# A two-layer mLSTM and band-attention trunk: row transfers on GpSimd's queue, transposes moved, key inputs scaled by VectorE, and splits put behind bank readers

## The chip, the cores and the metric

The kernel runs on one core of one Trainium2 chip. The metric is the device time of an execution in microseconds, as the median of several runs.

## The reference

The input is 512 tokens of width 2048. Layer 0 is an mLSTM layer with 8 heads, layer 1 attends in chunks of 64 over a band of nine chunks. The keys and values of layer 1 come from the residual stream after layer 0, normalised and modulated anew (`hkv`) and multiplied by `kv_w`. All is float32.

```python
def mlstm_mixer(h, w_in, conv_w, conv_b, gate_b, g_head, w_out):
    proj = h @ w_in
    qk = jax.nn.silu(causal_conv(proj[..., :A_V0].astype(F32), conv_w.astype(F32), conv_b.astype(F32)))
    ...
    gates = proj[..., A_G0:].astype(F32) + gate_b.astype(F32)
    ...
    ht = mlstm_chunkwise(heads(qk[..., :A_QK], A_DK), heads(qk[..., A_QK:], A_DK), heads(v, A_DV), li, lf)
    ht = rmsnorm(ht.transpose(0, 2, 1, 3), g_head.reshape(A_HEADS, A_DV)).reshape(Bn, S, A_INNER)
    y = jax.nn.sigmoid(o.astype(F32)) * ht * jax.nn.silu(z.astype(F32))
    return y.astype(h.dtype) @ w_out

def reference(...):
    for l in range(DEPTH):
        mod = sc @ ada_w[l].astype(F32) + ada_b[l].astype(F32)
        ...
        h = modulate(rmsnorm(x, g_pre[l]), shift, scale).astype(x.dtype)
        if l < N_A_LAYERS:
            y = mlstm_mixer(h, ...)
        else:
            if l == N_A_LAYERS:
                hkv = modulate(rmsnorm(x, kv_g), kmod[:, :D_MODEL], kmod[:, D_MODEL:]).astype(x.dtype)
                kv = hkv @ kv_w
            y = band_attention_mixer(h, k_sh, v_sh, ...)
        x = (x.astype(F32) + gate[:, None, :] * rmsnorm(y, g_post[l])).astype(x.dtype)
```

## The kernel before

Every float32 product is made from three: both factors are split into a high and a low part of the type fp32r (`split`, L247 and L248: ScalarE copies the high part, VectorE subtracts it to get the low one), and `mm` (L316) and `mm3` issue high by high, high by low and low by high into one bank of PSUM. The weights come in pieces of up to 128x1024 in the order in which they are used, always by a load on SP's queue (`raw_load`, L264, tile `wr`); `wpiece` splits a piece into `wh`, and for the projections by seven products (`proj_s`, L365) first forms sums of its blocks on VectorE (`ws`, L287 to L289), which are split into `wsh`. PE multiplies as soon as its piece is there, so PE, ScalarE and VectorE work at neighbouring pieces.

A scheduler sets the order of each engine by priorities. Code under `tc.high_priority(AHEAD)` is put ahead, `behind(a, b)` (L240) puts an instruction behind another in its engine's order without a wait, `pin` keeps program order. A projection takes a table `at` of functions that are called at step `k` of its loop over the 16 input tiles; that is how small work is laid beside products. On an engine, what stands behind a waiting instruction waits too.

The stages that the change touches, in the order of time:

- **Start (to 27 us).** Squares of the input are summed over tokens by PE (`token_sums`), `rc` and the reciprocal give the norm, PE spreads it (`ps_rb`), and the first row tile `h1t` can be made. `awake` (called at L642) issues products that nobody reads, two per call. `ada_sum` (L557) sums one column of the adaLN modulation on VectorE; `early[0]` and `early[1]` are two columns in two halves each, 128x1024.
- **Gates (211 to 250 us).** `gates` (L758) makes the gates' sums in `ps_g`, copies them to `g32`, selects input and forget gate by two products (`ps_li`, `ps_f`), runs log-sigmoid and two scans on VectorE and ScalarE, writes two rows to `gsc`, and transposes `ssum` (its rows `e`) into `aT` by PE (`ps_at`). Behind it head 0's `proj_b` makes the values (`ps_v`).
- **Output of layer 0 and K/V (1400 to 1850 us).** `rows` multiplies by `a_w_out`, in two pairs of row tiles for column groups 2 and 3; `evac` (L1177) multiplies a bank with the gate row `ssum` (loaded by `gate_row`, L1173). `residual` (L1210) adds the input rows and writes the result `y` to `xsc`. `turned` (L1228) normalises four columns' worth (`xn`), transposes them on PE into two banks (`ps_x`), copies each bank to `xk` on ScalarE and writes it to `nsc`. For the first pair of row tiles (`use` false) the key inputs are made later from `xk`, by `key_inputs`; for the second pair (`use` true) at once from the bank. `key_input` (L1220) scales and shifts in place on ScalarE, then splits into `hkv`. `values` (L1366) multiplies with `kv_w` (`ps_kv`) and writes the values to `vsc`. All of these writes and the gate rows are issued by SP.
- **Attention (from about 2040 us).** A head's query and gate come from `proj_s` with four banks D, C, A and B. At its end (L419 to L428) ScalarE reads D, then VectorE reads the banks in the order D, C, C, C, A, B. The next head's `proj_s` takes the banks in turn as they come free.
- **Tail.** `gate_part`, `gate_row(1, 0)` and `gate_first` prepare the last gate row beside `proj_b` of `b_w_out` (`gate_steps`, L1662).

## Time and profile before

| | |
|---|---|
| median of 3 runs | 2621.36 us (2617.01 to 2622.87) |
| profiled execution | 2618.51 us, span 2616.7 us |
| TensorE's clock over the span | 0.999 of full |
| PE busy | 2570.2 us |
| VectorE (DVE) busy | 2324.7 us |
| ScalarE (ACT) busy | 1418.5 us |
| GpSimd (POOL) busy | 57.9 us |

PE's busy time counts matrix products; DVE is VectorE, ACT ScalarE, POOL GpSimd, SP the engine that issues most transfers. An idle time in brackets stands ahead of the instruction that ended it, with what released it.

### The profile page before, as it was taken

Reading aid. Unit: us, or ns where it says so; the run is one execution under the profiler, and the core shown is the slowest. Engines: PE = TensorE matmul, PEld = TensorE weight load, DVE = VectorE, ACT = ScalarE, POOL = GpSimd, SP = SyncE. Lnnn points to the kernel's source line nnn. Section 1 sums busy time; section 2 is a strip of 40 time slices with the busy share of each in tenths; the row PEclk is TensorE's granted clock in tenths of the full one; section 3 lists DMA queues with packets and bytes.
Section 4 is the critical chain, followed back from the end, with each engine's and each line's share of the span. In section 5 each row is a group of like instructions: output and inputs, shape, how many; then the busy total and the mean of one; then the engine's idle time right before and its main releaser. Section 6 shows DMA issues by size and latency. Waiting matters only on the chain. (4 is left out here: it accounts for less than half of the span.)

```text
span 2616.7 us, 45705 instructions
## 1 busy us (share of the span) xinstructions
PE 2570.2 (98%) x17988; PEld 2404.6 (92%) x17988; DVE 2324.7 (89%) x3804; ACT 1418.5 (54%) x2096; POOL 57.9 (2%) x115
## 2 busy tenths in 40 slices
PE   8999999999999999999999999999999999999998
PEld 6887888899999999999999998888999899999887
DVE  8997899999999999999998886877997999999767
ACT  4335534565565555556655442478443776767523
POOL 0000111000000000000000000000000000000000
PEclk9999999999999999999999999999999999999999
DMA  9785597234333343333437558788654544444787
GB/s 366 316 346 198 211 395 297 94 109 141 113 100 135 109 134 112 106 130 114 125 127 249 182 172 330 256 290 282 227 177 145 170 129 145 133 136 134 255 298 251
DMA packets 154019, 506.15 MB, mean 193 GB/s; under 512 B 17750, under 2 KB 31606, under 8 KB 139338
## 3 DMA queue, kind: packets, MB, share of 16 engines
q1 hardware_dynamic: 143482, 442.58, 49.6%
q0 software_dynamic: 10320, 60.65, 6.2%
q8 instruction: 141, 2.31, 0.4%
q14 instruction: 76, 0.61, 0.1%
HBM read 469.50 MB, written 38.90 MB: 194 GB/s over the span
## 5 line engine op out<-in xcount | busy, mean ns | idle before, releaser
L248 ACT CAST wh<-wr 128x1024 fp32r<-128x1024 f32 (+1 forms) x528 | 544.9, 1034 | 483.9 <-DVE wr L288 104.3
L248 DVE TENSOR_TENSOR wh<-wr,wh 128x1024 fp32r<-128x1024 f32 (+1 forms) x528 | 636.3, 1208 | 134.4 <-ACT wh L248 133.5
L248 ACT CAST wsh<-ws 128x768 fp32r<-128x768 f32 (+1 forms) x296 | 241.3, 815 | 294.9 <-PE ps_az L316 60.9
L248 DVE TENSOR_TENSOR wsh<-ws,wsh 128x768 fp32r<-128x768 f32 (+1 forms) x296 | 277.6, 938 | 44.8 <-ACT wsh L248 43.7
L287 DVE TENSOR_TENSOR ws<-wr 128x512 f32<-128x512 f32 (+1 forms) x296 | 199.9, 678 | 8.2 <-DMA wr<-in_wst 7.8
L560 DVE CUSTOM_DVE_ANT_0 ada<-ada,scB,cl 128x2048 f32<-128x2048 f32 (+1 forms) x86 | 199.0, 2323 | 3.6 <-DMA ada<-in_adaT 3.3
L316 PE MATMUL ps_y<-wh,y 128*128 128x512 f32 x768 | 168.6, 380 | 0.0
L316 PE MATMUL ps_y_False<-wh,y 128*128 128x512 f32 x768 | 167.7, 380 | 0.8 <-DVE wh L248 0.8
L316 PEld LDWEIGHTS ps_y_False<-wh,y 128*128 128x128 f32 x768 | 144.5, 189 | 21.8 <-DVE wh L248 1.6
L316 PEld LDWEIGHTS ps_y<-wh,y 128*128 128x128 f32 x768 | 144.3, 189 | 20.7 <-DVE wh L248 0.4
L316 PE MATMUL ps_kv<-wh,hkv 128*128 128x512 f32 x576 | 128.5, 384 | 1.1 <-DVE wh L248 1.0
L316 PE MATMUL ps_v<-wh,h 128*128 128x512 f32 x576 | 127.6, 380 | 0.0
L289 DVE TENSOR_TENSOR ws<-wr 128x256 f32<-128x256 f32 (+1 forms) x296 | 123.5, 420 | 3.2
L316 PEld LDWEIGHTS ps_kv<-wh,hkv 128*128 128x128 f32 x576 | 109.0, 191 | 18.2 <-DVE wh L248 2.9
L288 DVE TENSOR_TENSOR wr<-ws,wr 128x256 f32<-128x256 f32 (+1 forms) x296 | 123.3, 419 | 2.5
L316 PEld LDWEIGHTS ps_v<-wh,h 128*128 128x128 f32 x576 | 108.2, 189 | 15.8 <-issue 0.9
L316 PE MATMUL ps_l<-h,wh 128*128 128x512 f32 x480 | 108.4, 381 | 3.0 <-DVE wh L248 2.1
L316 PEld LDWEIGHTS ps_l<-h,wh 128*128 128x128 f32 x480 | 90.0, 189 | 18.6 <-DVE wh L248 3.5
L316 PE MATMUL ps_azo<-h,wh 128*128 128x256 f32 (+1 forms) x606 | 92.9, 285 | 0.0
L316 PE MATMUL ps_y_True<-wh,y 128*128 128x512 f32 x384 | 83.3, 379 | 0.0
L316 PEld LDWEIGHTS ps_y_True<-wh,y 128*128 128x128 f32 x384 | 72.5, 189 | 10.2
L316 PEld LDWEIGHTS ps_azo<-h,wh 128*128 128x128 f32 x606 | 79.3, 192 | 1.1
(435 smaller groups left out, 5828.7 us busy)
## 6 DMA issues: line engine op xcount, KB each, us to landing
wr<-in_wst SPq DMA_DIRECT2D x498, 512.0 KB, 4.1
ada<-in_adaT POOLq DMA_DIRECT2D x54, 1024.0 KB, 8.6
ada<-in_adaT SPq DMA_DIRECT2D x52, 1024.0 KB, 7.0
ada<-in_adaT SPq DMA_DIRECT2D x36, 512.0 KB, 6.2
wr<-in_wst SPq DMA_DIRECT2D x26, 384.0 KB, 7.5
xt<-nsc SPq DMA_DIRECT2D x32, 256.0 KB, 3.2
yr<-ysc SPq DMA_DIRECT2D x28, 256.0 KB, 5.3
ysc<-zo SPq DMA_DIRECT2D x24, 256.0 KB, 4.5
```

The lines of the kernel that those rows point to most:

```text
L248: ins = nc.scalar.copy(hi, src), nc.vector.tensor_tensor(lo, src, hi.bitcast(F32), op=ALU.subtract)
L287: nc.vector.tensor_tensor(t[:, : 2 * w], r[:, w : 3 * w], r[:, : 2 * w], op=ALU.subtract)
L288: nc.vector.tensor_tensor(r[:, w : 2 * w], t[:, w : 2 * w], r[:, :w], op=ALU.add)
L289: nc.vector.tensor_tensor(t[:, 2 * w :], r[:, 3 * w :], r[:, w : 2 * w], op=ALU.subtract)
L316: product[0] = nc.tensor.matmul(ps, a, b, start=start, stop=stop)
L560: pin(nc.vector.tensor_tensor_reduce(c, c, (sc or scB)[:, j * w : (j + 1) * w], 1.0, mod[:, i : i + 1] if j else col(CB + i), ALU.mult, AL ...
```

## The change

1. The idle pair after the third quarter of the input goes; the first half of `early[1]`'s sum comes ahead of the reciprocal, the second behind the copy of `ps_rb`.
2. `gates` is cut in three: sums and copy (with priority), `gate_rows` at step 2 of head 0's `proj_b`, `gate_cols8` (the transposes) at step 12. Head 0's mask tiles are loaded behind that projection.
3. Layer 0's gate rows, the writes to `xsc` and `nsc`, and those to `vsc` of groups 0 and 1 are issued by GpSimd: 6 loads of `ssum` and 16, 16 and 8 writes, 46 transfers.
4. `key_input` scales on VectorE in place, adds the shift with the rounding copy on ScalarE, and gets the low part by one VectorE instruction that adds the shift and subtracts the high part.
5. `turned` for the first pair moves from steps 8 and 14 of group 2 and 4 and 10 of group 3 to step 10 of group 2 and 0, 6, 12 of group 3; for the second pair from 4, 8, 14 to 4, 10, 14. Its copy and key inputs have priority where the second pair uses them at once.
6. In head 1's `proj_s` the low split of piece 1 and the first block sum of piece 2 are put behind head 0's last reader of bank C (`emptied`), and so are the low splits of the tiles that were kept plain.
7. In the tail three gate steps move by two steps each, and one to the last pair.

```diff
-            nc.vector.tensor_tensor(t[:, : 2 * w], r[:, w : 3 * w], r[:, : 2 * w], op=ALU.subtract)
+            summed[0] = nc.vector.tensor_tensor(t[:, : 2 * w], r[:, w : 3 * w], r[:, : 2 * w], op=ALU.subtract)
...
+        if held_back and i in (1, 2):
+            behind((parted[0], summed[0])[i - 1], emptied[0])
...
-        nc.vector.tensor_tensor(z(z2, 1), z(z1, 1), c1, op=ALU.add)
+        emptied[0] = nc.vector.tensor_tensor(z(z2, 1), z(z1, 1), c1, op=ALU.add)
...
-def ada_sum(i, at, w, js, pin=lambda ins: ins, sc=None):
+def ada_sum(i, at, w, js, pin=lambda ins: ins, sc=None, j0=None):
+    j0 = js[0] if j0 is None else j0
...
-        c = at[:, (j - js[0]) * w : (j - js[0] + 1) * w]
+        c = at[:, (j - j0) * w : (j - j0 + 1) * w]
...
-    if q:
+    if q in (1, 3):
...
+ada_sum(*early[1][:3], [0], pin)
...
-ada_sum(*early[1], pin)
+ada_sum(*early[1][:2], early[1][2], [1], pin, None, 0)
...
-    nc.scalar.copy(like(g32[:32], S), read(g_ps[:32], S))
+    with tc.high_priority(AHEAD):
+        nc.scalar.copy(like(g32[:32], S), read(g_ps[:32], S))
+    return g32
+
+def gate_rows(g32):
...
+
+def gate_cols8():
+    e = ssum[:8]
...
-        gates()
+        g32 = gates()
...
-    nm = hp.tile([P, S], F32, tag="nm", name=f"nm{h}")
-    nmd = hp.tile([P, 4, P], F32, tag="nmd", name=f"nmd{h}")
-    nc.sync.dma_start(nm, gsc[0, h].partition_broadcast(P))
+
+    def mask_tiles():
+        nm = hp.tile([P, S], F32, tag="nm", name=f"nm{h}")
+        nmd = hp.tile([P, 4, P], F32, tag="nmd", name=f"nmd{h}")
+        nc.sync.dma_start(nm, gsc[0, h].partition_broadcast(P))
+        return nm, nmd
...
+        nm, nmd = mask_tiles()
...
+        add_at(at, {2: lambda: gate_rows(g32), 12: gate_cols8})
...
+        nm, nmd = mask_tiles()
...
-    nc.sync.dma_start(gb, ggd[layer, 4 * g : 4 * g + 4, :].rearrange("k p -> (k p)").partition_broadcast(P))
+    (nc.sync if layer else nc.gpsimd).dma_start(gb, ggd[layer, 4 * g : 4 * g + 4, :].rearrange("k p -> (k p)").partition_broadcast(P))
...
-        nc.sync.dma_start(xsc[m, :, d], y)
+        nc.gpsimd.dma_start(xsc[m, :, d], y)
...
-    nc.scalar.activation(tmp, tmp, AF.Identity, bias=mod[:, 96 + k : 97 + k], scale=amul[:, KT + k : KT + k + 1])
+    shift = mod[:, 96 + k : 97 + k]
+    nc.vector.tensor_scalar(tmp, tmp, amul[:, KT + k : KT + k + 1], None, op0=ALU.mult)
...
-    split(hkv[k][:, 0, t], hkv[k][:, 1, t], tmp)
+    hi, lo = hkv[k][:, 0, t], hkv[k][:, 1, t]
+    nc.scalar.activation(hi, tmp, AF.Identity, bias=shift)
+    nc.vector.scalar_tensor_tensor(lo, tmp, shift, hi.bitcast(F32), op0=ALU.add, op1=ALU.subtract)
...
-            nc.scalar.copy(keep, ps)
+            with tc.high_priority(AHEAD if use else 0):
+                nc.scalar.copy(keep, ps)
...
-            nc.sync.dma_start(nsc[k : k + 2, :, t].rearrange("a p t -> p a t"), keep)
+            nc.gpsimd.dma_start(nsc[k : k + 2, :, t].rearrange("a p t -> p a t"), keep)
...
-            if use:
-                for j in range(2):
+            with tc.high_priority(AHEAD if use else 0):
+                for j in range(2 if use else 0):
...
-            at |= {8 + 6 * i: lambda i=i: turned(0, [i], False) for i in range(2)}
+            at[10] = lambda: turned(0, [0], False)
...
-            at = {4 + 6 * i: lambda i=i: turned(0, [2 + i], False) for i in range(2)}
+            at = {6 * i: lambda i=i: turned(0, [1 + i], False) for i in range(3)}
...
-        nc.sync.dma_start(vsc[g][:, :, m * P : (m + 1) * P], v.rearrange("p (j t) -> p j t", j=4))
+        (nc.gpsimd if g < 2 else nc.sync).dma_start(vsc[g][:, :, m * P : (m + 1) * P], v.rearrange("p (j t) -> p j t", j=4))
...
-        turn = {k: lambda i=i: turned(1, [i], True) for i, k in enumerate((4, 8, 14))} if pair == 0 and g == 1 else {}
+        turn = {k: lambda i=i: turned(1, [i], True) for i, k in enumerate((4, 10, 14))} if pair == 0 and g == 1 else {}
...
-    proj_s("b_w_in", h2, h2s, ATT_PAIRS if h else ATT_FIRST, z1, z2, f"z{h}", kq, (2, 2), steps, True, late=True)
+    proj_s("b_w_in", h2, h2s, ATT_PAIRS if h else ATT_FIRST, z1, z2, f"z{h}", kq, (2, 2), steps, True, late=True, held_back=h == 1)
...
-                split(s1[:, 0, :], s1[:, 1, :], raw[0][:, 256:])
+                behind(split(s1[:, 0, :], s1[:, 1, :], raw[0][:, 256:])[0], emptied[0])
...
-    3: {2: lambda: (gate_row(1, 3), fetch_x(3)), 6: lambda: gate_part(0), 8: lambda: gate_row(1, 0, late[1]), 12: lambda: gate_first(0), 14: lambda: gate_first(2)},
+    3: {2: lambda: (gate_row(1, 3), fetch_x(3)), 8: lambda: gate_part(0), 10: lambda: gate_row(1, 0, late[1]), 14: lambda: gate_first(0)},
...
-        at = {4: lambda: finish(0), 6: lambda: finish(1)} if pair == PAIRS[1] else {}
+        at = {2: lambda: gate_first(2), 4: lambda: finish(0), 6: lambda: finish(1)} if pair == PAIRS[1] else {}
```

How the order moves, at three places. PE at the gates, before: `ps_v0` are head 0's values, `wh41` the weight piece.

```order
L316 MATMUL ps_g_1593<-h1_15_1338,gw_1540 32x512 x2
L316 MATMUL ps_v0_0_1668<-wh41_1674,h1_0_269 128x512 x3
L316 MATMUL ps_v0_0_1668<-wh41_1674,h1_1_302 128x512
L316 MATMUL ps_li_1628<-g32_1626,kcs_101 8x512
L316 MATMUL ps_f_1629<-g32_1626,kcs_101 8x512
L316 MATMUL ps_v0_0_1668<-wh41_1674,h1_1_302 128x512 x2
```

And after the change:

```order
L316 MATMUL ps_v0_2_1633<-wh41_1637,h1_1_301 128x512 x3
L316 MATMUL ps_v0_3_1634<-wh41_1637,h1_0_268 128x512 x3
L316 MATMUL ps_v0_3_1634<-wh41_1637,h1_1_301 128x512 x3
L316 MATMUL ps_li_1664<-g32_1625,kcs_101 8x512
L316 MATMUL ps_f_1665<-g32_1625,kcs_101 8x512
L316 MATMUL ps_v0_0_1631<-wh42_1693,h1_2_392 128x512 x3
L316 MATMUL ps_v0_1_1632<-wh42_1693,h1_2_392 128x512 x3
```

The two selecting products moved from behind four products of `wh41` to behind all 24 of them. The transposes `ps_at` stood within `wh44` and stand behind `wh46`:

```order
L316 MATMUL ps_v0_1_1632<-wh46_1812,h1_11_931 128x512 x3
L316 MATMUL ps_v0_2_1633<-wh46_1812,h1_11_931 128x512 x3
L316 MATMUL ps_v0_3_1634<-wh46_1812,h1_11_931 128x512 x3
L804 MATMUL ps_at_1842<-kcs_101,ssum_108 128x8 x4
L316 MATMUL ps_v0_0_1631<-wh47_1850,h1_12_1041 128x512 x3
L316 MATMUL ps_v0_1_1632<-wh47_1850,h1_12_1041 128x512 x3
```

VectorE where layer 0's second pair of rows begins its last column group, before: `xn` are normalised rows, `ps_y0_2_2` and `ps_y0_2_3` banks to be evacuated, `wh338` and `wh339` splits.

```order
L1236 TENSOR_SCALAR xn0_3_17984<-y0_3_16628,rsn_107 128x512
L1236 TENSOR_SCALAR xn1_3_17986<-y1_3_16678,rsn_107 128x512
L248 TENSOR_TENSOR wh338_17878<-wr338_17876,wh338_17878 128x1024
L1179 TENSOR_TENSOR ps_y0_2_2_False_17610<-ps_y0_2_2_False_17610,y2_2_16142 128x512
L1183 TENSOR_TENSOR y2_2_16142<-ps_y0_2_2_False_17610,ssum_108 128x512
L1179 TENSOR_TENSOR ps_y0_2_3_False_17611<-ps_y0_2_3_False_17611,y3_2_16192 128x512
L1183 TENSOR_TENSOR y3_2_16192<-ps_y0_2_3_False_17611,ssum_108 128x512
L248 TENSOR_TENSOR wh339_17919<-wr339_17917,wh339_17919 128x1024
```

After the change:

```order
L1256 TENSOR_SCALAR xn0_3_18007<-y0_3_16627,rsn_107 128x512
L1256 TENSOR_SCALAR xn1_3_18009<-y1_3_16677,rsn_107 128x512
L1241 TENSOR_SCALAR xk0_0_17749<-xk0_0_17749,amul_104 128x256 x2
L248 TENSOR_TENSOR wh338_17877<-wr338_17875,wh338_17877 128x1024
L1196 TENSOR_TENSOR ps_y0_2_2_False_17609<-ps_y0_2_2_False_17609,y2_2_16141 128x512
L1196 TENSOR_TENSOR ps_y0_2_3_False_17610<-ps_y0_2_3_False_17610,y3_2_16191 128x512
L1200 TENSOR_TENSOR y2_2_16141<-ps_y0_2_2_False_17609,ssum_108 128x512
L1200 TENSOR_TENSOR y3_2_16191<-ps_y0_2_3_False_17610,ssum_108 128x512
L248 TENSOR_TENSOR wh339_17898<-wr339_17896,wh339_17898 128x1024
L1246 SCALAR_TENSOR_TENSOR hkv0_17868<-xk0_0_17749,mod_103,hkv0_17868 128x256
L1241 TENSOR_SCALAR xk0_2_17757<-xk0_2_17757,amul_104 128x256 x2
```

The two scalings of `xk0_0` stand ahead of `wh338` and of the evacuations.

VectorE at the end of attention's head 0, before: `wh430`, `ws431` and `wr431` are head 1's weights, `z0` and `zq0` head 0's results, `ps_dz0` and `ps_cz0` the banks D and C.

```order
L248 TENSOR_TENSOR wsh429_0_22026<-ws429_0_22019,wsh429_0_22026 128x768
L248 TENSOR_TENSOR wh430_22077<-wr430_22071,wh430_22077 128x1024
L287 TENSOR_TENSOR ws431_0_22147<-wr431_22145 128x512
L248 TENSOR_TENSOR h2_14_21736<-xt14_0_21683,h2_14_21736 128x256
L288 TENSOR_TENSOR wr431_22145<-ws431_0_22147,wr431_22145 128x256
L420 TENSOR_TENSOR z0_21751<-zq0_21750,ps_dz0_21752 128x256
L289 TENSOR_TENSOR ws431_0_22147<-wr431_22145 128x256
L421 TENSOR_TENSOR zq0_21750<-z0_21751,ps_cz0_21753 128x256
L422 TENSOR_TENSOR z0_21751<-z0_21751,ps_cz0_21753 128x256
L423 TENSOR_TENSOR z0_21751<-zq0_21750,ps_cz0_21753 128x256
```

After the change:

```order
L248 TENSOR_TENSOR wsh429_0_22025<-ws429_0_22018,wsh429_0_22025 128x768
L422 TENSOR_TENSOR z0_21750<-zq0_21749,ps_dz0_21751 128x256
L423 TENSOR_TENSOR zq0_21749<-z0_21750,ps_cz0_21752 128x256
L424 TENSOR_TENSOR z0_21750<-z0_21750,ps_cz0_21752 128x256
L425 TENSOR_TENSOR z0_21750<-zq0_21749,ps_cz0_21752 128x256
L248 TENSOR_TENSOR wh430_22076<-wr430_22070,wh430_22076 128x1024
L426 TENSOR_TENSOR zq0_21749<-zq0_21749,ps_az0_21753 128x512
L428 TENSOR_TENSOR z0_21750<-z0_21750,ps_bz0_21754 128x512
L248 TENSOR_TENSOR wsh430_0_22079<-ws430_0_22072,wsh430_0_22079 128x768
```

The four readers of D and C come first, head 1's split `wh430` behind them, its next weight steps behind those of A and B.

## Rows read from the trace of the kernel before

**Rows 1.** The page, part 1: busy us of each engine, share, instructions.

```profile
PE 2570.2 (98%) x17988; PEld 2404.6 (92%) x17988; DVE 2324.7 (89%) x3804; ACT 1418.5 (54%) x2096; POOL 57.9 (2%) x115
```

**Rows 2.** Waits of PE, whole run: line, releaser; us in total, times, longest.

```profile
PE ps_li L316 <- ACT g L764: 2.3, 1, 2.3
PE ps_gg L839 <- DVE ggate L837: 1.5, 1, 1.5
PE ps_at L793 <- DVE ssum L784: 1.4, 1, 1.4
PE ps_x L1244 <- DVE xn L1236: 1.4, 2, 0.7
```

**Rows 3.** Timeline 16 to 28 us: start, us, instruction, idle before and its releaser.

```profile
17.73 1.20 PE L316 MATMUL ps_idle<-scB,cst 128*128 128x256 f32 x2
22.47 0.18 DVE L648 RECIPROCAL rc<-rc 128x4 f32<-128x4 f32 x1 [2.23 <-ACT rc L645]
22.57 1.25 DVE L560 CUSTOM_DVE_ANT_0 ada<-ada,scB,cl 128x1024 f32<-128x1024 f32 x1
25.44 0.75 DVE L529 SCALAR_TENSOR_TENSOR h1t<-xt,amul,ps_rb 128x512 f32<-128x512 f32 x1 [0.28 <-ACT ssum L655]
```

**Rows 4.** Timeline 209 to 250 us, around the gates.

```profile
213.45 0.56 ACT L764 COPY g<-ps_g 32x512 f32<-32x512 f32 x1
...
244.31 1.23 DVE L248 TENSOR_TENSOR wh<-wr,wh 128x1024 fp32r<-128x1024 f32 x1 [3.95 <-ACT wh L248]
...
248.81 0.55 POOL L554 DMA_DIRECT2D ada<-in_adaT  x1 [4.05 <-DVE mod L560]
```

**Rows 5.** Timeline 1707 to 1720 us, where layer 0's rows are turned.

```profile
1708.01 1.08 ACT L1248 COPY xk<-ps_x 128x512 f32<-128x512 f32 x2 [0.42 <-PE ps_x L1244]
...
1709.61 1.28 DVE L1236 TENSOR_SCALAR xn<-y,rsn 128x512 f32<-128x512 f32 x3
...
1710.10 0.95 SPq L1250 DMA_DIRECT2D nsc<-xk  x2
1710.30 1.04 PE L1244 MATMUL ps_x<-kcs,xn 128*128 128x128 f32 x8
...
1711.10 8.02 PE L316 MATMUL ps_y_False<-wh,y 128*128 128x512 f32 x36
...
1715.95 0.60 ACT L1223 ACTIVATE xk<-xk,mod,amul 128x256 f32<-128x256 f32 x1 [3.38 <-DMA nsc<-xk]
```

**Rows 6.** Timeline 2082 to 2086 us, where attention's second head begins.

```profile
2082.39 0.36 ACT L419 COPY zq<-ps_dz 128x256 f32<-128x256 f32 x1
2082.51 1.22 DVE L248 TENSOR_TENSOR wh<-wr,wh 128x1024 fp32r<-128x1024 f32 x1
...
2084.91 0.42 DVE L420 TENSOR_TENSOR z<-zq,ps_dz 128x256 f32<-128x256 f32 x1
...
2085.39 0.94 PE L316 MATMUL ps_cz<-h2s,wsh 128*128 128x256 f32 x6 [2.82 <-DVE z L420]
```

**Rows 7.** Timeline 1743 and 1773 us: two waits of PE.

```profile
1743.49 1.78 PE L316 MATMUL ps_kv<-wh,hkv 128*128 128x512 f32 x7 [0.62 <-DVE wh L248]
...
1773.25 0.95 PE L1244 MATMUL ps_x<-kcs,xn 128*128 128x128 f32 x4 [2.44 <-DVE hkv L248]
```

**Rows 8.** Windows: length; busy PE, PEld, DVE, ACT, POOL; clock, DMA share, GB/s.

```profile
1740.00:1750.00 10.00, 9.38 (x44) 7.93 (x43) 10.00 (x19) 8.57 (x20) 0.00 (x0) 1.00 0.67 209
...
1770.00:1774.00 4.00, 1.56 (x11) 1.21 (x9) 2.93 (x7) 4.00 (x10) 0.00 (x0) 0.93 0.91 245
1774.00:1784.00 10.00, 10.00 (x46) 8.56 (x45) 5.94 (x9) 6.55 (x13) 0.00 (x0) 0.86 0.66 206
```

**Rows 9.** DMA issues: queue, count, KB each, median us from issue to landing.

```profile
ada<-in_adaT POOLq DMA_DIRECT2D x54, 1024.0 KB, 8.6
...
out<-yo POOLq DMA_DIRECT2D x8, 256.0 KB, 4.0
out<-yo SPq DMA_DIRECT2D x8, 256.0 KB, 2.7
```

More of the change, by code (lines that the diff above doesn't have):

```diff
@@ L311, in wpiece @@
         return out
-    product = [None]
+    product, emptied, summed = [None], [None], [None]
     def mm(ps, a, b, start, stop):
@@ L363, in proj_b, with proj_s @@
             held.clear()
-    def proj_s(mat, xs, ss, f, z1, z2, name, pl, bufs, at={}, merged=False, banks="pppp", lead=AHEAD, late=False):
+    def proj_s(mat, xs, ss, f, z1, z2, name, pl, bufs, at={}, merged=False, banks="pppp", lead=AHEAD, late=False, held_back=False):
         D, C, A, B = [(newa if b == "a" else newp)(f"ps_{n}{name}") for n, b in zip("dcab", banks)]
```

## The prediction

> **What bounds the kernel now.** I read the page's busy times first, then PE's waits over the whole run, then the timeline at the places that the change touches, then the windows for the clock. PE is busy for 2570.2 of 2616.7 us [rows 1], so everything a reordering can win is the 46.5 us in which it is not, plus what a fallen clock costs. A gain counts only where PE stands and the changed step is what it stands for. The waits on the change's own lines are few and each has one place [rows 2]: the gates' first product on ScalarE's copy (2.3 us), the gates' transposes on the chain behind it (1.4), two waits on the normalised rows (1.4 together). Two larger ones lie in the attention and in the shared K/V stage (below). The sum is made against the profiled execution's 2618.5 us, which lies 2.9 below the median of the three runs, 2621.4; a time is given as a median by adding the 2.9 again. About 0.2%, or 5.2 us, is what a measurement of this kernel can tell from no change.
>
> **Start.** One idle pair goes, which held PE for about 1.0 us at 17.73 ahead of the last token sums. The reciprocal at 22.47 ended 2.23 us of VectorE idleness, so VectorE was free at 20.24 [rows 3]. The first half of the adaLN sum (1.25) now goes there and ends at 21.5, just where the reciprocal could start if its input comes 1.0 earlier. VectorE's 0.28 at 25.44 stays a wait for the same copy, which comes earlier too. Gain 0.9; between 0, if the stage that follows is held by its weight loads, and 2.0, if VectorE's 2.2 us of filled idleness is passed on to PE.
>
> **Gates.** ScalarE's copy of the gate sums ends at 213.45 + 0.56 = 214.01 [rows 4], and PE had stood for it for 2.3 us [rows 2], from about 211.7. The product now stands behind 20 further matmuls. Thirty-six of that shape took 8.02 us, 0.223 each [rows 5], so PE gets there 4.5 us later, at 216.2, when the copy is done. The transposes move behind 57 more matmuls, 12.7 us. Their chain starts about 2.2 later than it did (216.2 against 214.01), so some 10 us are in hand over a wait of 1.39. That chain's scans now push the weight splits behind them, but one of these stood 3.95 us for ScalarE at 244.31 [rows 4], so a few us of delay are covered there; if the cover is gone, PE stands at a split instead. Gain 2.30 + 1.39 = 3.7; ends 1.5 (the second wait returns at a split) and 3.7.
>
> **Attention.** PE stood 2.82 us at 2085.39 for the first reader of a bank, which VectorE reached only at 2084.91, behind 1.22 us of head 1's split and three smaller weight steps [rows 6]. ScalarE's copy, which that reader needs, ends at 2082.75. The reader now comes first: 2082.75 + 0.42 = 2083.2, so PE starts 2.2 us earlier. What is late next is head 1's split: it ends at about 2085.6, and PE needs it after 30 of the short matmuls, six of which take at most 0.94 us [rows 6], so 3 to 4.7 us after 2083.2, from 2086.5 on. Two pieces later the splits have hardly any slack, because the scores' operand is now split behind more weight steps, so I take 2.0, with ends 0.8 and 2.8.
>
> **K/V stage.** At 1773.25 PE stood 2.44 us for a bank that key_input had not yet emptied [rows 7], and the granted clock fell to 0.93 and then 0.86 in the windows around it, a mix of 2.4 GHz with some 1.2 GHz, right after that stand [rows 8]: 10 us at 0.86 lose 1.4. The second set of transposes now comes two steps, 12 matmuls or 2.7 us, later, just over the 2.44, and copies and key inputs have priority, so the wait goes and with it, I take it, the fall. Gain 2.44 + 1.4 = 3.8; ends 1.0 (the third set now follows the second after four steps where it had six, and meets the same banks) and 4.2. The 32 scalings that VectorE gains are 128x256. By the 128x512 row (1.28 for three, 0.43 each [rows 5]) that is 0.21 each, and up to 0.42 for those in PSUM, by the equally small row at 2084.91 [rows 6]: 7 to 13 us over a stage where VectorE is idle for over a third of the time (8.87 busy of 14 us from 1770 on [rows 8]). Only 1740 to 1750 is full (10.00 of 10 [rows 8]); PE stood 0.62 there [rows 7], and two such scalings add 0.5. ScalarE's relief is worth nothing there, since VectorE ends last.
>
> **The writes on POOL.** This is the cost that the trace of before does not show. Forty-six transfers leave SP for POOL. The scaling is in place, so it must wait until the write of the same tile to nsc has landed, and now VectorE waits, in its order, ahead of a weight split and of the next evacuations. Before, ScalarE waited: 3.38 us, released at 1715.95 by a write that SP issued at 1710.10, thus 5.85 later [rows 5]. Now the first of the two copies ends at about 1708.6, POOL's issue takes 0.55 [rows 4], and with 5.85 the landing comes 6.4 after the copy, at 1715.0. VectorE is there at 1709.61 + 1.28 = 1710.9 and stands for 4.1 us. Its split then ends at 1715.0 + 0.4 + 1.25 = 1716.65. PE wants it at 1711.10 + 24 x 0.223, less the 0.8 that the transposes moved behind it take (1710.30 to 1711.10) [rows 5]: 1715.65. So PE loses L - 5.4 us there, with L the time from copy to landing: 1.0 at L = 6.4. For the three later pairs VectorE comes some 5.6 us after the copy and has about 1 us in hand over PE, L - 6.6 each, nothing at 6.4. The bounds of L are 4.0 + 0.55, POOL's 256 KB writes of the output, and 8.6 + 0.55, its 1 MB loads [rows 9]; I take SP's figure for the same write, the nearest row. Cost 1.0; ends 0 and 11.4 (3.75 + 3 x 2.55).
>
> The rows of the output's writes speak for a longer L: the same 256 KB took 4.0 on POOL and 2.7 on SP [rows 9], 1.3 more; with 1.3 more here L is 7.7 and the cost 2.3 + 3 x 1.1 = 5.6. A page of the Trainium skill gives a reason against such a move, "SBUF — State Buffer", section "SBUF: two separate sides": GpSimd writes the descriptors of its own DMAs through a port pair that VectorE locks in its two-port modes, and a transfer of 0.62 us alone took 3.1 beside a copy. By that, an estimate, L would be 2.5 longer, 8.9, the cost 10.4 and the time 2621.9. The trace bears out a lengthening of about half that size.
>
> **Steps that I cost at nothing.** The two waits on normalised rows (1.4 [rows 2]) stay: those transposes keep their place in PE's order. The tail's moved gate steps leave every engine's order as it was, so the 1.5 us for the gate row [rows 2] stays too. SP, freed of 46 issues, may bring a weight load forward; no wait of PE in this stage names one.
>
> **Sum.** 0.9 + 3.7 + 2.0 + 3.8 - 0.5 - 1.0 = 8.9 us, so 2609.6 for a profiled execution and 2612.5 as a median.
>
> **Rivals.**
> First, waits that only move: a split behind the gates' chain, head 1's later splits, the third set of transposes. For it speaks that each was covered by only 1 to 4 us of idleness; against it, that the gates' transposes have 10 us in hand. All three at their low ends give 0.9 + 1.5 + 0.8 + 1.0 - 1.5 = 2.7 us: 2618.7, no change that can be told.
> Second, POOL's writes land late while VectorE is busy, between L = 7.7 (the 1.3 of [rows 9]) and the upper bound, 9.15. The whole is then worth 9.9 - 5.6 = 4.3, or 9.9 - 11.4 = -1.5: 2617.1 to 2622.9. For it: POOL was the slower queue in the one pair of rows that compares them; against it: 1.3 is a figure of another stage. The Trainium skill's rule on the shared ports belongs here; its figure lies inside this span.
> Third, the same mechanism carried to the other side, slower: four stands of VectorE, each with a PE stall and a fallen clock behind it. Without the landings the change is worth 9.9. It turns at 4L = 35.1, L = 8.8, and is slower by 5.2 from L = 10.1 on. At L = 10.5 the time is 5.1 + 3 x 3.9 = 16.8 lost, net 6.9: 2628.3. For it: DMA share is 0.91 in the neighbouring window [rows 8], and a 1 MB load on POOL needs 8.6. Against it: these writes are a quarter of that size, and one was seen at 5.85.
> Fourth, the change does not do what it says: for the tail that is so by the order; for the rest the order shows the moves.
>
> **How the numbers follow.** My forecast, the sum with single terms off by one or two us but at least 5.2 in all, 0.66. First rival 0.13. Second 0.14, all of it within 0.2%. Third 0.07. Faster by over 0.2%: 0.66; within: 0.27; slower: 0.07. The forecast's own range is 2607 to 2616, from the high ends of the terms (2.0 + 3.7 + 2.8 + 4.2 = 12.7, and 1.7 for the spread of single runs, which before's show to be larger) to 5.2. The range to hold 8 in 10 takes in the first rival and most of the second: 2607 to 2621.
>
> **What would show it.** Right: no wait of PE on the gates' copy or transposes; PE's wait at the attention's second head down to about 0.6; no wait of PE for a bank near 1773 and a clock of 1.00 there; VectorE standing 3 to 5 us for an nsc write at the first scaling and 0 to 2 at the three others, with PE losing about 1. Wrong: VectorE stands of 6 us and more there; a new wait of PE for a weight split near 235 to 245 or 2090 to 2097; a clock below 1.00 between 1710 and 1740.

## The result, and the profile after

The change made the kernel slower: 2625.45 us as the median of 12 runs (2622.65 to 2629.74) against 2621.36 of 12 runs of the kernel before beside them, ratio 1.0019 with a 95% interval of 1.0011 to 1.0026. Forecast were 2612.5, and 2607 to 2621. The profiled execution has a span of 2623.5 us.

The page's part 1 of the kernel after, to be read against [rows 1]:

```profile
PE 2571.8 (98%) x17986; PEld 2405.1 (92%) x17986; DVE 2335.8 (89%) x3836; ACT 1405.5 (54%) x2063; POOL 87.4 (3%) x161
```

PE is as busy as before, in a span 6.8 us longer; VectorE has 11.1 us more, within the 7 to 13 that were worked out. PE's waits, whole run, as [rows 2]:

```profile
PE ps_kv L316 <- DVE wh L248: 5.1, 7, 1.3
PE ps_x L1264 <- ACT sqy L1203: 3.2, 1, 3.2
PE ps_kv L316 <- ACT wh L248: 2.7, 2, 2.5
PE ps_t L1550 <- DVE s L1541: 2.3, 2, 1.5
...
PE ps_kv L316 <- ACT hkv L1245: 1.6, 1, 1.6
PE ps_gg L850 <- DVE ggate L848: 1.5, 1, 1.5
PE ps_x L1264 <- DVE xn L1256: 1.3, 3, 0.8
```

The waits on the gates' copy and transposes are gone, as is that of attention's bank; those on the tail and on the normalised rows stay, as forecast. New are the waits of the K/V stage (`ps_x` on a square sum, `ps_kv` on weights). Three markers show where the time went. The view of one line's instructions gives their first and last start: the gate of the output norm (first at 294, last at 2584), layer 0's evacuations, and the first keys. Before:

```profile
L837 DVE TENSOR_TENSOR ggate<-mod,cl x5: 155/159/165, 299.3 to 2576.8; 128x4 f32<-128x4 f32 x4, 128x16 f32<-128x16 f32 x1
L1183 DVE TENSOR_TENSOR y<-ps_y_False,ssum x16: 681/684/692, 1604.3 to 1741.6; 128x512 f32<-128x512 f32 x16
L426 DVE TENSOR_TENSOR zk<-zk,ps_bk x2: 679/682/684, 1855.3 to 1875.5; 128x512 f32<-128x512 f32 x2
```

After:

```profile
L848 DVE TENSOR_TENSOR ggate<-mod,cl x5: 154/155/162, 294.0 to 2584.2; 128x4 f32<-128x4 f32 x4, 128x16 f32<-128x16 f32 x1
L1200 DVE TENSOR_TENSOR y<-ps_y_False,ssum x16: 678/682/683, 1599.3 to 1742.9; 128x512 f32<-128x512 f32 x16
L428 DVE TENSOR_TENSOR zk<-zk,ps_bk x2: 679/679/679, 1863.6 to 1883.9; 128x512 f32<-128x512 f32 x2
```

The change is 5.3 us ahead at the first gate and 5.0 at the first evacuation, and 8.3 behind at the first keys: the stage from evacuation to keys takes 264.3 us where it took 251.0, 13.3 more. From the first keys to the last gate it wins 0.9 (720.6 against 721.5). So all of the loss lies in the output and K/V stage. Between its two markers PE stands 16.3 us (264.30 - 248.01) where it stood 6.2 (251.00 - 244.79). The windows of before and after (columns as [rows 8]):

```profile
1604.30:1855.30 251.00, 244.79 (x1217) 213.03 (x1216) 197.93 (x285) 160.16 (x275) 0.00 (x0) 0.99 0.84 283
```

```profile
1599.30:1863.60 264.30, 248.01 (x1213) 213.01 (x1212) 209.44 (x317) 149.94 (x243) 28.92 (x45) 0.99 0.78 268
```

The first part of the loss, in the timeline at 1704 to 1716 us (start, duration, instruction, idle before and its releaser; answers to [rows 5]):

```profile
1703.94 1.08 ACT L1269 COPY xk<-ps_x 128x512 f32<-128x512 f32 x2
...
1704.96 1.60 POOL L1271 DMA_DIRECT2D nsc<-xk  x2 [3.57 <-ACT xk L1269]
...
1711.09 0.62 DVE L1241 TENSOR_SCALAR xk<-xk,amul 128x256 f32<-128x256 f32 x2 [4.28 <-ACT wh L248]
...
1711.62 1.22 DVE L248 TENSOR_TENSOR wh<-wr,wh 128x1024 fp32r<-128x1024 f32 x1
...
1713.95 1.28 DVE L1200 TENSOR_TENSOR y<-ps_y_False,ssum 128x512 f32<-128x512 f32 x2
1714.73 0.58 ACT L1203 ACTIVATE sqy<-ps_y_False 128x512 f32<-128x512 f32 x1 [3.72 <-DVE y L1200]
...
1715.47 1.12 PE L1264 MATMUL ps_x<-kcs,xn 128*128 128x128 f32 x4 [3.25 <-ACT sqy L1203]
```

The first copy ends at 1704.52 (1703.94 + 0.58), the scaling runs at 1711.09: L is 6.6, forecast 6.4, and VectorE stands 4.28 us (4.1). The row names ScalarE's cast, which ended at 1711.00, but the scaling does not read what that cast wrote. What it needs is the write issued at 1704.96, and the view of that write alone says 6.0 us from issue to landing, thus 1711.0:

```profile
DMA to landing us min/median/max: 6.0/6.0/6.0
```

Behind the scaling stand the split and the four evacuation steps, behind these ScalarE's square sum, which is the last reader of a bank, and for that bank PE's next transposes stand 3.25 us. At the later pairs VectorE stands four more times, up to 3.52, and behind the longest PE stands 1.25 for the split that follows the scaling:

```profile
1739.40 0.61 DVE L1241 TENSOR_SCALAR xk<-xk,amul 128x256 f32<-128x256 f32 x2 [3.52 <-DMA nsc<-xk]
...
1741.21 2.86 PE L316 MATMUL ps_kv<-wh,hkv 128*128 128x512 f32 x12 [1.25 <-DVE wh L248]
```

The second part of the loss is near 1800. Windows of the kernel after (columns as [rows 8]):

```profile
1710.00:1720.00 10.00, 6.75 (x30) 5.68 (x29) 8.35 (x14) 5.51 (x12) 1.97 (x3) 0.83 0.54 189
...
1800.00:1810.00 10.00, 7.00 (x30) 5.23 (x29) 5.28 (x11) 6.50 (x10) 0.73 (x1) 1.00 0.95 345
1810.00:1820.00 10.00, 9.38 (x36) 7.97 (x37) 9.93 (x16) 8.63 (x13) 0.71 (x1) 0.83 0.65 217
```

PE loses some 3 us of 10 in two windows, and the granted clock is 0.83, a mix of 2.4 and 1.2 GHz, in the window of the first stand and in the one behind the second: an estimate of up to 2 x 10 x 0.17 = 3.4 us. Before, in [rows 8], the clock fell in this stage only behind the 2.44, by the same reckoning 4 x 0.07 + 10 x 0.14 = 1.7 us.

### The profile page after: what moved, and what is told of

It reads as the page before. It is cut to its first block, busy times and chain, and to the rows that moved or that the text cites. A ratio compares the mean times of both kernels' runs of the same rounds, so it can differ in the third digit from the quotient of the medians.

```text
span 2623.5 us, 45740 instructions
## 1 busy us (share of the span) xinstructions
PE 2571.8 (98%) x17986; PEld 2405.1 (92%) x17986; DVE 2335.8 (89%) x3836; ACT 1405.5 (54%) x2063; POOL 87.4 (3%) x161
## 4 chain that ended last, share of the span: by engine, by line
PE 67%; DVE 21%; issue 7%; DMA 2%; ACT 2%; POOL 1%; SPq 0%; DVEq 0%; ACTq 0%; POOLq 0%
PE ps_y L316 6%; DVE wh L248 5%; PE ps_azo L316 4%; PE ps_czo L316 4%; PE ps_dzo L316 4%; PE ps_y_True L316 3%; PE ps_az L316 3%; PE ps_y_False L316 3%; PE ps_dz L316 3%; PE ps_cz L316 3%; PE ps_o L316 3%; DVE wsh L248 2%; PE ps_l L316 2%; PE ps_v L316 2%; PE ps_bzo L316 2%
## 5 line engine op out<-in xcount | busy, mean ns | idle before, releaser
L316 PEld LDWEIGHTS ps_y_True<-wh,y 128*128 128x128 f32 x384 | 72.6, 189 | 10.2
```

The source lines that it names most:

```text
L316: product[0] = nc.tensor.matmul(ps, a, b, start=start, stop=stop)
```

## Experiments

Times are medians; a ratio is to the kernel before, run beside it; "us of the ratio" is its distance from 1 times 2621.4, and gains and costs below are told in it. For the change itself that is +5.0. The edits are given in short form, with several places of the code in one line.

**Which part.** The change without parts 3 to 5: `key_input`, `turned` and the issues as before.

```diff
-scale on VectorE; turned at {10}, {0, 6, 12}, (4, 10, 14); nc.gpsimd
+scale on ScalarE; turned at {8, 14}, {4, 10}, (4, 8, 14); nc.sync
```

> The change without its K/V part: transfers of layer 0 on SP, key_input on ScalarE, transposes at their old steps, no priority for copies and key inputs. Theory (all of the loss lies in the K/V stage, between pieces 300 and 380 of the weights): start and gates keep their 5 us, the attention its 1, so 5 to 7 us below before, ratio about 0.9975. Rival (the gates' or the attention's part shifts work that costs time later): 0 to 3 us below before.

2617.08, 0.9974 [0.9962, 0.9985]: start, gates, attention and tail are worth 6.8 us. The reverse, the kernel before with parts 3 to 5 alone:

```diff
-scale on ScalarE; turned at {8, 14}, {4, 10}, (4, 8, 14); nc.sync
+scale on VectorE; turned at {10}, {0, 6, 12}, (4, 10, 14); nc.gpsimd
```

> The kernel before with the K/V part alone (transfers on GpSimd, key inputs scaled by VectorE, moved transposes, priorities). Theory: 9 to 13 us above before, ratio 1.004 to 1.005. Rival (the loss needs the shift of 5 us that the earlier parts bring): under 4 us.

2634.16, 1.0039 [1.0026, 1.0052], 10.2 us slower. With the earlier parts the same parts cost 11.8 (5.0 + 6.8), so the loss does not need them. Then the whole change, but all 46 transfers back on SP:

```diff
-nc.gpsimd.dma_start(xsc / nsc / vsc / gate row ...)
+nc.sync.dma_start(...)
```

> The change with all 46 transfers back on SP; scaling in place on VectorE and moved transposes kept. Theory A (the in-place scaling makes VectorE wait for the landing, whichever queue issued the write; SP's write lands 5.9 us after its issue, GpSimd's was waited for some 6.5 us): PE still stands 2 us and more for a bank near 1712, and 0 to 3 us are won on the change. Theory B (GpSimd's queue is the cost): 8 to 12 us are won, 4 to 8 below before, and no wait of PE there.

2613.26, 0.9958 [0.9945, 0.9972]: 11.0 us faster than before. So parts 4 and 5 are worth 4.2 (11.0 - 6.8; the two intervals overlap), and the issues by GpSimd cost 16 us, 0.0061 of the ratio (13 by the medians; these intervals lie well apart). PE's waits from 1650 to 1860 us in this run:

```profile
PE ps_kv L316 <- DVE wh L248: 2.5, 3, 1.0
PE ps_kv L316 <- ACT hkv L1245: 0.9, 1, 0.9
PE ps_x L1264 <- ACT wh L248: 0.8, 1, 0.8
```

No wait for a bank is left, neither the 2.44 of [rows 7] nor the 3.25. The same without the order that part 6 sets:

```diff
-proj_s(..., late=True, held_back=h == 1)
+proj_s(..., late=True)
```

> All transfers on SP (as in the run before that did so), and in the attention head 1's splits no longer held behind head 0's bank readers. Theory (holding wins PE's 2.8 us at the second head, but gives part back at the softmax's transposes): 0 to 2 us slower than with the hold, PE again standing 2 to 3 us for z, and no wait for the softmax's rows. Rival (the hold is worth its full 2 us and more): 2 to 3 us slower.

2615.36, 0.9971 [0.996, 0.9982]. That is 3.4 us for part 6 (1.8 by the medians), but the two intervals overlap, so the size is open. What is plain in the trace is that without it PE stands again, and the clock behind it falls (timeline and window):

```profile
2079.48 1.65 PE L316 MATMUL ps_cz<-h2s,wsh 128*128 128x256 f32 x6 [2.19 <-DVE z L422]
```

```profile
2080.00:2090.00 10.00, 10.00 (x77) 9.94 (x76) 9.49 (x17) 6.15 (x9) 0.00 (x0) 0.87 0.27 83
```

**Which transfers.** One group on GpSimd, the others on SP. The nsc writes alone:

```diff
-nc.gpsimd.dma_start(xsc / vsc / gate row ...)
+nc.sync.dma_start(...)
```

> The change with only the 16 nsc writes on GpSimd; gate rows, xsc and vsc writes back on SP. Theory A (the nsc writes are what is waited for): nearly the whole loss stays, 0 to 3 us won on the change. Theory B (46 transfers in one queue delay each other, the nsc writes behind the xsc and vsc writes): 5 us and more are won, and the wait for nsc at the first scaling is under 2 us.

2619.88, 0.9985 [0.9976, 0.9994], 8.9 better than the change, though the stand at the first scaling is still there: 4.95 us of VectorE, and 4.00 of PE for the square sum's bank. Neither expectation fits whole. The values' vsc writes alone:

```diff
-nc.gpsimd.dma_start(xsc / nsc / gate row ...)
+nc.sync.dma_start(...)
```

> The change with everything on SP (2613.3) but the 8 writes of the values to vsc, which GpSimd issues as in the change. The run with the nsc writes alone on GpSimd (2619.9) was about 6 us faster than the change, most of it between 1800 and 1850. If the values' writes are what costs there (their landings, or the order that they bring about): 2617 to 2619.5, with PE waits for weight splits of 2 us and more near 1807. If the gate rows and xsc writes are: 2612.5 to 2614.5, with the K/V stage as in the run with all on SP. If the loss comes only where these writes and the nsc writes share GpSimd's queue: 2612.5 to 2614.5 here and in the next run as well.

2617.5, 0.9985 [0.9977, 0.9994]. The gate rows and xsc writes alone:

```diff
-nc.gpsimd.dma_start(nsc / vsc ...)
+nc.sync.dma_start(...)
```

> The change with everything on SP (2613.3) but the 6 gate rows and the 16 writes to xsc, which GpSimd issues as in the change. If these cost the 6 us: 2617 to 2619.5, and then a wait of PE for a normalised row or a load of the rows must show between 1690 and 1850. If the values' writes do, or only the sharing of the queue with the nsc writes: 2612.5 to 2614.5.

2616.76, 0.9984 [0.9975, 0.9993]. Each group costs about 7 us against all on SP, with intervals clear of that run's; all three cost 16, less than the sum. The last two expectations had set one group against the other; both cost. Moving only the second pair's eight nsc writes back to SP changes nothing that can be told:

```diff
-nc.gpsimd.dma_start(nsc ...)
+(nc.sync if use else nc.gpsimd).dma_start(nsc ...)
```

> The change with only the second pair's eight nsc writes back on SP. PE's order is the same as the change's. Theory A (the loads of nsc for the attention's input wait for GpSimd's late writes, and ScalarE and VectorE stand for those loads ahead of weight splits): the losses from 1800 to 1850, some 9 us, shrink to under 3, so 5 to 8 us are won on the change; PE's 3.25 us near 1712 stay. Theory B (the loss there comes from the values' writes or from the key inputs' priority): under 2 us.

2626.81, 1.0013 [1.0004, 1.0022]; its first expectation had 5 to 8 us won on the change.

**The nsc writes: landing or order.** First the wait taken away: the first pair's key inputs are scaled into a tile of their own.

```diff
-nc.vector.tensor_scalar(tmp, tmp, ...)
+src, tmp = tmp, rows_p[0].tile([P, w], F32, tag="ks", bufs=1)
+nc.vector.tensor_scalar(tmp, src, ...)
```

> The change with the scaled key input of the first pair written to a scratch tile of its own, so that VectorE need not wait for the write of the tile it reads; transfers on GpSimd. Theory A (the wait for the landing behind the in-place scaling): PE's 3.25 us near 1712 and the low clock after it go, 4 to 6 us are won on the change; the losses from 1800 to 1850 stay. Theory B (GpSimd's queue in general, or the places of the transposes): under 2 us are won.

2621.81, 0.9994 [0.9984, 1.0004], 6.6 us better than the change; PE's wait for the square sum is gone, though PE now stands 1.85 us for a normalised row, up to 1704.59. Then only the order: the first two scalings behind the evacuations, where the kernel with all on SP has them (`emptied` is the last evacuation).

```diff
+behind(scaled, emptied[0])
```

> The change, transfers on GpSimd, but VectorE's first two scalings are put behind the evacuations and weight splits that they stood ahead of, as the scheduler itself places them when SP issues the writes. Theory A (VectorE's place in the order: the scheduler takes GpSimd's writes for landed earlier than they are): PE's 3.25 us near 1712 go and 4 to 6 us are won on the change, as with the scratch tile; the losses from 1800 to 1850 stay. Theory B (GpSimd's queue slows the stage by itself): under 2 us are won.

2624.21, 1.0008 [0.9999, 1.0017], 2.9 better by intervals that overlap, less than the 4 to 6 expected; the 3.25 is gone here too, but PE stands 2.71 us for a normalised row, up to 1705.88. And a step towards the reverse: all on SP, with the split put behind the scaling (`parted` is that split).

```diff
+behind(parted[0], scaled)
```

> The change with everything on SP, and weight split 338 put behind the first scaling on VectorE, as it stands in the change. It tells the order from the queue at 1712. If the order that came with GpSimd is what costs there: PE loses 2 to 4 us near 1712 as in the change (a wait for the square sum's bank or for the split), clock below 1.00 behind it, 2615.5 to 2618. If it is GpSimd's later landing in itself, SP's write lands about 1 us sooner, and PE loses at most 1: 2612.5 to 2615.

2614.46, 0.9971 [0.996, 0.9982], 3.4 us worse than all on SP, with SP's landings. The median falls into the second expectation's range; that PE stands 1.49 us for the split, up to 1714.26, and 1.32 up to 1730.56 speaks for the first. It is not the change's order, though: here three of the four evacuation steps stand ahead of the scaling, in the change all four behind it, and no wait for the square sum's bank shows. PE's longest item from 1650 to 1860 us:

```profile
PE ps_y_False L319 <- DVE wh L248: 3.4, 3, 1.5
```

So this order would be up to half of the 7 us that the nsc writes cost; the intervals of 0.9971 and 0.9958 overlap, so this share is not certain. That the scheduler puts the scaling ahead because its own reckoning frees SP is argued, not shown; the run with gate rows and xsc writes on GpSimd, below, fits it.

**The values' writes: the ring.** In the run with vsc alone on GpSimd, SP's waits and ScalarE's, 1780 to 1850 us:

```profile
SPq L1289 <- DMA vsc<-v: 16.1, 5, 5.4
```

```profile
ACT xt L1423 <- DMA xt<-nsc: 13.7, 7, 3.6
```

With all on SP they were

```profile
SPq L1289 <- DMA vsc<-v: 1.7, 3, 0.7
```

```profile
ACT xt L1423 <- DMA xt<-nsc: 7.0, 7, 2.7
```

The values' tiles `v` share a ring of six buffers with the row tiles `xt`. SP's load of the next `xt` waits until the write of an old `v` has landed, now by another queue, and weight loads stand behind it on SP. The landing is late because GpSimd issues the second of two values' writes late. Timelines of GpSimd in this run, and of SP with all on SP:

```profile
1805.72 0.72 POOL L1399 DMA_DIRECT2D vsc<-v  x1 [20.09 <-ACT v L1398]
1811.47 0.71 POOL L1399 DMA_DIRECT2D vsc<-v  x1 [5.03 <-issue]
```

```profile
1802.65 0.52 SPq L1399 DMA_DIRECT2D vsc<-v  x1
...
1804.35 0.53 SPq L1399 DMA_DIRECT2D vsc<-v  x1
```

The second tile was ready at 1807.03 in the first and its write was issued 4.4 us later. It stood for the first write: the view of that one, issued at 1805.72, gives the time to its landing, thus 1811.2, and the second starts 0.3 us after it.

```profile
DMA to landing us min/median/max: 5.5/5.5/5.5
```

If this is the way, buffers of their own must win it back (`vp` is a pool of four):

```diff
-v = tp.tile([P, S], F32, tag="t", ...)
+v = vp.tile([P, S], F32, tag="v", ...)
```

> As the run with the values' writes alone on GpSimd (2617.5), but the values of groups 0 and 1 have four buffers of their own, not the ring of six that the row tiles use. If SP's stand for those writes (16.1 us, five times, up to 5.4) is the way in which they cost: SP's waits on vsc are gone, ScalarE's waits for rows fall from 13.7 to about 7, and the time is 2610 to 2614. If the later landing costs in another way, or the order of the half sums does: 2616 to 2619.

2613.04, 0.9956 [0.9943, 0.9968], all of the 7 us back, and the interval is clear of the other's. SP's loads of rows wait for no vsc write, and ScalarE's waits for rows are

```profile
ACT xt L1423 <- DMA xt<-nsc: 3.4, 3, 2.3
```

**Gate rows and xsc writes.** On VectorE this run too has the scaling ahead of the split, though its nsc writes are SP's. With the two scalings put behind the evacuations:

```diff
+behind(scaled, emptied[0])
```

> As the run with the gate rows and xsc writes alone on GpSimd (2616.8), but the first two scalings put behind the evacuations on VectorE, where they stand with all on SP. If the order that came with fewer issues on SP is what costs: 2611 to 2614, and no wait of PE for a square sum's bank near 1716. If GpSimd's landings or issues do: 2615.5 to 2618.

2614.71, 0.9966 [0.9952, 0.9979], 4.7 of the 6.8 us won back, PE's wait for the square sum down from 0.8 to 0.4. That speaks for order, but the two intervals overlap, and a longer stand went with it that the order of the scalings does not explain: in the run before PE stood 1.85 us for a normalised row, up to 1707.00, behind a cast that had waited 2.18 for its weight load; here the two are 0.44 and 0.59.

**All together.** The whole change with both buffers:

```diff
+the key inputs' tile "ks" and the values' pool vp, as above
```

> The whole change, all 46 transfers on GpSimd, with two additions: the first pair's scaled key inputs in a tile of their own (alone 2621.8), and the values in four buffers of their own. If the loss goes through these two buffers: 2611 to 2616. If it lies in the landings or the order as such: 2618 to 2622.

2623.16, 1.0005 [0.9995, 1.0016]: no better than the first of the two alone, a miss. The expectation took the two ways for the whole of the loss. The timeline near 1703 shows another. All on SP, with the tile of its own:

```profile
1699.03 1.05 ACT L248 CAST wh<-wr 128x1024 fp32r<-128x1024 f32 x1 [1.00 <-DMA wr<-in_wst]
...
1708.35 0.50 SPq L1224 DMA_DIRECT2D xr<-in_xN  x1
```

The whole change with both buffers:

```profile
1701.44 1.84 SPq L1224 DMA_DIRECT2D xr<-in_xN  x2
...
1703.25 1.05 ACT L248 CAST wh<-wr 128x1024 fp32r<-128x1024 f32 x1 [2.84 <-DMA wr<-in_wst]
1704.20 0.59 ACT L1233 ACTIVATE sqx<-y 128x512 f32<-128x512 f32 x1
...
1706.73 0.87 PE L1267 MATMUL ps_x<-kcs,xn 128*128 128x128 f32 x6 [2.37 <-DVE xn L1259]
```

and the windows 1700 to 1710 of the two, in that order:

```profile
1700.00:1710.00 10.00, 9.34 (x47) 7.95 (x46) 9.02 (x17) 5.30 (x10) 0.00 (x0) 1.00 0.97 289
```

```profile
1700.00:1710.00 10.00, 7.02 (x32) 5.47 (x31) 7.12 (x15) 4.40 (x9) 2.55 (x4) 0.90 1.00 374
```

SP, which no longer waits for each `y` to write it, issues the residual loads `xr` 7 us earlier, into the time of GpSimd's writes; 374 GB/s move where 289 did (328 in the kernel before), the next weight load lands late, and the cast that waits for it holds back the square sum and the rows that PE wants. Two runs on this. The xsc writes and gate rows back on SP, the rest on GpSimd with both buffers:

```diff
-nc.gpsimd.dma_start(xsc / gate row ...)
+nc.sync.dma_start(...)
```

> The change with both buffers of their own (2623.2), and with the gate rows and the xsc writes back on SP; the nsc writes and the values' writes stay on GpSimd. If the rest of the loss comes from the queue that SP's loads no longer share with the xsc writes: 2612 to 2616, and no stand of PE over 1.2 us for normalised rows near 1704. If the nsc writes on GpSimd cost it (their landings, or SP's stands for them, 10.0 us): 2618 to 2622.

2615.35, 0.9984 [0.9975, 0.9992], 5.5 us won. And all on GpSimd, with the residual loads behind the xsc writes on the same queue:

```diff
-nc.sync.dma_start(xrs[m][g], ...)
+nc.gpsimd.dma_start(xrs[m][g], ...)
```

> The change with both buffers of their own (2623.2), all 46 transfers on GpSimd, and the residual loads xr as well, so that those of the last row tile stand behind the xsc writes of the first two. If the loads that overtake are what holds the weights back near 1703: no stand of PE over 1.2 us for normalised rows near 1704, 2616 to 2620 (the stands after 1750 stay). If not: 2621 to 2625 with the stand in place.

2620.71, 1.0002 [0.9992, 1.0012]: the stand at 1704 is gone (the longest wait for a normalised row is now at 1749),

```profile
PE ps_x L1267 <- DVE xn L1259: 2.7, 3, 1.5
```

but the time is the same within the intervals (1.0005 and 1.0002). PE now stands 1.75 us up to 1747.75 for a key input and 1.54 up to 1750.63 for a normalised row, and the clock from 1750 to 1760 is 0.66, where it was 0.83 in the run with both buffers. So the early residual loads made that stand, but that they cost time is not shown. What remains in both runs, some 7 us against all on SP in the former, stays open. The former's trace names SP's waits for the second pair's nsc writes,

```profile
SPq L1292 <- DMA nsc<-xk: 11.1, 4, 3.8
```

none of which stand there with all on SP: the row loads read what those writes put down. And these writes are late for the same reason as the second values' write, since both kinds share GpSimd's queue:

```profile
1779.37 0.73 POOL L1402 DMA_DIRECT2D vsc<-v  x1 [5.45 <-ACT v L1401]
1780.05 0.76 POOL L1274 DMA_DIRECT2D nsc<-xk  x1
1786.13 0.73 POOL L1274 DMA_DIRECT2D nsc<-xk  x1 [5.33 <-ACT xk L1272]
```

The vsc write landed 6.5 us after its issue, at 1785.8. The second nsc write, whose tile was ready at 1779.9, started 0.3 us behind that landing. Whether this is all of what remains was not tried.

**A better version.** That is all on SP. With the tile "ks" of its own it does not get faster clear of noise:

> The change with everything on SP, and the first pair's key inputs scaled into a tile of their own, so that no scaling waits for a write to nsc. If the stands of VectorE for these writes (5.3 us in the run with all on SP, longest 2.4) are covered, as that run's waits of PE say: 2612.0 to 2614.5. If they still cost PE through late splits or clock: 2609 to 2611.5.

2610.88, 0.9958 [0.9945, 0.997], and with the pool `vp` for the values besides:

> The change with everything on SP, scaled key inputs in a tile of their own (2610.9 so far), and the values in four buffers of their own. SP stood only 1.7 us for vsc there: 2609 to 2612 if that wait was covered; below 2609 if more room in the ring helps the row loads; slower than 2612.5 if row loads that come earlier push weight loads back on SP.

2613.82, 0.9963 [0.995, 0.9975]. The medians fall into the ranges "still cost PE" and "slower", but by the ratio both are no different from the change with all on SP (0.9958), so SP's landings were covered there as far as these runs can tell. These, and the run with own buffers and vsc on GpSimd (0.9956), beat both kernels by 0.4 to 0.6%.

## Why the prediction was wrong

**Start: right.** `h1t` starts at 24.82 where it started at 25.44 [rows 3], 0.6 of the 0.9.

**Gates: right.** Both waits are gone. Start and gates together are 5.3 us by the first gate's marker, forecast 4.6.

**Attention: right.** From the first keys to the last gate, all on SP wins 2.0 (719.5 us against 721.5), as forecast; the change 0.9, near the low end: PE stands 2.3 us in all for the transposes of the attention weights, on VectorE's scaling of them, where it stands 1.5 with all on SP and not at all before. The text named another late next step, the splits. (Its sum has a slip that changes no term: 3 us after 2083.2 is 2086.2, not 2086.5.) Parts 1, 2, 6 and 7 were forecast at 6.6 (part 7 at nothing) and measured 6.8.

**K/V stage and scalings: right.** 3.8 - 0.5 = 3.3 forecast, 4.2 measured, by intervals that overlap. The 2.44 and the fallen clock behind it are gone with all on SP; without parts 3 to 5 PE stands 2.34 there.

**The writes on POOL: the term that failed.** Forecast 1.0 with ends 0 and 11.4; measured 16. L was right, 6.6. Three steps failed. First, "PE loses L - 5.4 us there" followed the one weight split behind the scaling. By it 1.2 were due. Behind the split stand the evacuations, and a bank that their square sum empties: 3.25, and a clock of 0.83 in that window. For the later pairs the text had "nothing at 6.4", because VectorE would come 5.6 us behind the copy. At the last it came 1.7 behind it, stood 3.52 and PE 1.25, though L was only 5.2. Secondly, the term held the 16 nsc writes and no others. The vsc writes cost 7 us through the ring that they share with the row tiles, and the gate rows and xsc writes 7, of which the order of the first scalings may be the most; each is as much as nsc. Thirdly, under the steps costed at nothing: "SP, freed of 46 issues, may bring a weight load forward". In the traces it was not weight loads that came forward: the first scalings moved ahead of a split and of the evacuations, and residual loads came 7 us and more earlier, with a weight load late behind them.

**The rivals.** The third, slower, named four stands of VectorE with L of 10.1 and more. It came out slower with L at 6.6 and less, so that mechanism is not what happened, and that its outcome came true is luck. Of the signs of being wrong, the clock below 1.00 between 1710 and 1740 came; stands of VectorE of 6 us and a late split at the gates or at attention's second head did not. The second, late landings, took its L from the output's rows (1.3 longer on POOL [rows 9]); the medians to landing, all on SP against the change from 1650 to 1850 us, are 4.6 and 5.3 (nsc), 5.4 and 5.7 (xsc), 4.8 and 5.1 (vsc), so 0.3 to 0.7 longer. That is from issue to landing; it leaves out the time that a vsc write stands on GpSimd ahead of its issue, up to 5 us, which the text did not know of. The lengthening of 2.5 worked out from the Trainium skill ("SBUF — State Buffer", section "SBUF: two separate sides") is not seen in them.

## What to carry to other kernels

When transfers leave a queue, look at what that queue and the scheduler do with the freed time: list the order of all engines around it, and for each moved write whose buffer or bank it releases and what stands behind that waiter on every engine, not only the next split. A queue that is shared also holds optional loads back; two queues let these compete with weight loads (seen here, though its cost is not shown), and a load on one queue that needs a buffer whose write is on the other stops all that stands behind it. Count the pieces of the writes that GpSimd issues in a row: a write can stand there until an earlier one has landed. Move one group of transfers at a time, and try the rest of the change without any first: here it was 0.4% faster than before, and 0.6% faster than with the move.

## What was not expected of the hardware

Two vsc writes of 256 KB in a row on GpSimd start 4.9 to 6.1 us apart, in each of the four pairs of the run with vsc alone there, and the second starts 0.30 to 0.42 us after the first has landed. On SP two start within 1.7 us. Two nsc writes of the same size take GpSimd 1.42 to 1.60 together, without such a stand.

The kinds differ in the number of their pieces: a vsc write is 512 of 128 numbers, an nsc write 256 of 256, an xsc write 128 of 512. Added up over the transfers that GpSimd had under way between 1380 and 1900 us, in all runs with such transfers, the sum was never above 896 pieces (seven loads of 128, in the run with the residual loads on GpSimd). An issue that would have made it 1024 stood until an earlier transfer had landed: vsc behind vsc (512 + 512), nsc behind vsc and nsc (512 + 256 + 256), the eighth load of 128 behind seven. Neither the bytes nor the number of transfers tells these apart, since all are of 256 KB and seven of the xr loads go together. So in these traces GpSimd's queue stands at 1024 pieces under way. No run was made to test it, with longer pieces for vsc for example.
